# A gated hybrid decoder layer on one core: w2 split at load, attention outputs fetched by background tasks, one more empty turn per attention head

## The chip, the core and the metric

The kernel runs on one core of a Trainium2 chip. The metric is the device time of one execution in microseconds, the median over several; a lower one is better. Engines are named as in the profile: PE is TensorE (with PEld for its weight loads), DVE VectorE, ACT ScalarE, POOL GpSimd and SP SyncE, which here only issues DMAs.

## What is computed

One decoder layer on 256 tokens of width 2048, all in fp32. Two token mixers work side by side: a gated linear attention (branch a) and a causal differential attention of 16 heads (branch b). Cut to what matters:

```python
h = rmsnorm(x, pre_norm_g)
a_q, a_k, a_v, a_g, a_lr, b_q, b_k, b_v, b_g, m_a, m_b = split(h @ w_in)
gk  = log_sigmoid(a_lr @ w2 + gk_b) / 16            # forget gate, w2: 16 x 1024
o_a = rmsnorm(gla_chunked(a_q, a_k, a_v, gk)) * silu(a_g)
o_b = rmsnorm(diff_attention(b_q, b_k, b_v, lam)) * silu(b_g)
y   = sigmoid(m_a) * (o_a @ w_branch_a) + sigmoid(m_b) * (o_b @ w_branch_b)
out = x + rmsnorm(y @ w_out, post_norm_g)
```

## The kernel before

**Products by halves.** Every fp32 operand is split into a high part, rounded to the format that TensorE takes in one pass, and a low part, the remainder. A product is hi·hi + hi·lo + lo·hi. Weights are split as they arrive: SP loads a raw tile of 1 MB (two units), then for each unit ACT writes hi (L298, or L259 for the blocks below) and DVE lo = raw − hi (L299, L260). This runs four units ahead of TensorE (`take` emits the next). The raw tiles, hi and lo come from a pool of three buffers each, so a load waits until DVE has finished with a tile three back.

**Stages.** Weights come in chunks, in the order of `schedule()`: v0 to v4 (the values of branch a and, in v0 to v3, the 32 columns of a_lr), k and q, ag (gates of a), dv, bg, dq, dk (branch b), m (merge gates), y00 to y03 (o_a times w_branch_a), y10 to y13 (o_b times w_branch_b), o (w_out). `token_major` (L444) walks a chunk's kt, with tokens' columns as the stationary operand, 12 matmuls of up to 512 columns a unit (L458; 416 columns in v1 to v3, 400 in v4); `channel_major` (L469) does dq and dk (L479, L481). Five pieces of the projection, the sets, are done with seven products in place of eight, each of four units called blocks: 6 matmuls of 512 columns a block (L658). Their weights come in by POOL's DMAs, which add in flight (L211), by DVE adds (L229) and a few SP loads (raw_s, L253). `mixed(n, keys)` strews n blocks evenly among the units of the named chunks; `alone(4)`, which the kernel has had nowhere in use before the change, puts four with no unit between.

**Background tasks.** Everything else is written as Python generators in a list `tasks`. `pump(n)` (L433) advances each of the first n tasks by one turn, up to its next `yield`; `token_major` pumps after each odd unit, and `block_set` after each odd block (L661). What a turn issues on PE stands behind the last product there. The order in each engine's queue is then a scheduler's, by the program's dependences; DMAs made through `fetch` (L724) keep their program order on SP. A DMA at the head of SP's queue that must wait holds all that stand behind it.

**The forget gate** (L506 to L547) is such a task. w2 lies four times in w2_raw, at rows 0, 32, 64 and 96, 128 rows in all. Its first turn splits them: ACT copies rows 0 to 63 into w2_s as high parts (L509), rows 64 to 127 into a tile w2h (L510), and DVE subtracts to get low parts in rows 64 to 127 of w2_s (L511; the profile calls w2_s w_s). The second turn transposes a_lr on PE (L515), and splits it to lrt (ACT L518, L520, DVE L522); the third issues the eight gate matmuls (L530) and copies their results out (ACT L533). The evacuation of a v chunk is L557 on ACT (vh) and L558 on DVE (vl), and frees its banks.

**Attention of branch b** (L991 to L1038) is one task of one head a turn or two: scores (L940, L941), softmax (DVE L945, ACT L951), a `yield`, the difference of the two maps (DVE L957 to L961, tile prob), a `yield`, its transposes (PE L966), and then for the head before: the product with the values (L972 to L974), the norm (ACT L982, DVE L984 to L989), and every second head transposes and a split. Each four heads' result is stored to DRAM as obh_far and obl_far by POOL's DMAs (L1028), as branch a's did as oah_far and oal_far; both are fetched again as the stationary operands of y0 and y1: oah, oal (four tiles each; kt 0, 1 use tile 0, kt 2, 3 tile 1, kt 8 and 9 tile 2, kt 10 and 11 tile 3) and obh, obl (tile kt/4). The tiles come from one pool of 34 buffers ("u").

**Fetches before.** After m12, m13 and the end of all tasks, the eight of oah and oal stand in a row (L1106 to L1109), then y00 to y03; then the eight of obh and obl (L1117 to L1121), then y10.

Of the kernel before, what the change touches and what calls it, by code (L numbers as in the profile page):

```python
# [7 lines left out]
F32R = mybir.dt.float32r  # L8
BF16 = mybir.dt.bfloat16
U8 = mybir.dt.uint8  # L10
AF = mybir.ActivationFunctionType
# [68 lines left out]
def schedule():  # L80

    kinds = {key: kind for key, kind, _, _ in chunk_plan()}
    steps = []
    blocks = [(i, n) for i in range(len(SETS)) for n in range(SLOTS * 4)]

    def regular(*keys):
        steps.extend((key, n) for key in keys for n in range(units(kinds[key])))

    def mixed(n, *keys):
        at = len(steps)  # L90
        regular(*keys)
        r = steps[at:]
        del steps[at:]
        for i, step in enumerate(r):
            steps.extend(blocks[: (i + 1) * n // len(r) - i * n // len(r)])
            del blocks[: (i + 1) * n // len(r) - i * n // len(r)]
            steps.append(step)

    def channels(g):
        return [key for key in kinds if key[:2] in ("dq", "dk") and key[2] == str(g)]  # L100

    order = [key for key, _, _, _ in chunk_plan()]
    def alone(n):
        steps.extend(blocks[:n])
        del blocks[:n]

    regular(*order[: order.index("v4")])
    mixed(SLOTS * 4, *order[order.index("v4") : order.index("ag0")])
    regular(*order[order.index("ag0") : order.index("dq10")])
    mixed(18, *channels(1))  # L110
    mixed(18, *channels(2))
    mixed(18, *channels(3))
    mixed(14, "m12", "m13")
    mixed(4, "y00")
    mixed(28, *(f"y0{g}" for g in range(1, 4)))
    mixed(12, "y10", "y11")
    regular("y12", "y13", *(f"o{g}" for g in range(4)))
    assert not blocks
    return steps
# [26 lines left out]
def hybrid_kernel(ctx: ExitStack, tc, xt, xn, preg, postg, w, w2, gkb, glag, lamv, diffg, ident_d, causal_d, lmask_d, out):  # L146
# [12 lines left out]
    def u(shape, name, dtype=F32):  # L159
        count[0] += 1  # L160
        return big.tile(shape, dtype, tag="u", name=f"{name}_{count[0]}")
# [17 lines left out]
    def f32(ap):  # L179
        return ap.bitcast(F32)  # L180
# [176 lines left out]
    def load_constants():  # L357
        for i in range(4):
            tc.keep_in_program_order(sp.dma_start(w2_raw[32 * i : 32 * i + RANK, :], w2))
        tc.keep_in_program_order(sp.dma_start(ident, ident_d))  # L360
        for t, src in ((gkb_s, gkb), (glag_s, glag), (diffg_s, diffg), (causal, causal_d)):
            tc.keep_in_program_order(sp.dma_start(t, src))
        tc.keep_in_program_order(sp.dma_start(lam_s, lamv.partition_broadcast(P)))
        yield
        for n in range(0, len(LEVELS) + 2, 4):
            m = min(4, len(LEVELS) + 2 - n)
            t = u([P, 4, S], "lmask")
            tc.keep_in_program_order(sp.dma_start(t[:, :m, :], lmask_d[:, n : n + m, :]))
            pool.tensor_copy(lmask[:, n : n + m, :], t[:, :m, :])
            yield  # L370
# [58 lines left out]
    DONE = object()  # L429
    done = set()  # L430
    latest = [None]

    def pump(n=1):  # L433
        with tc.issue_after(latest[0]):
# [9 lines left out]
    def token_major(key, n, ops, step=1, groups=1):  # L444
        banks = [[ps(tag), ps(tag)] for tag in ("mm", "bg")[:groups]]
        spots = [(g, b) for g in range(groups) for b in range(2)]
        rows = 2 // groups
        for q in range(KT // rows):
            hi, lo = take(key)
            for w, parts in ((hi, (0, 1)), (lo, (0,))):  # L450
                for j in range(rows):
                    kt = rows * q + j
                    a = ops(kt)
                    for g, b in spots:
                        c = n * (groups * j + g)
                        for part in parts:
                            first, last = kt == 0 and w is hi and part == 0, kt == KT - 1 and w is lo
                            i = pe.matmul(banks[g][b][:, :n], a[part][:, P * b : P * b + P], w[:, c : c + n], start=first, stop=last)  # L458
            latest[0] = i.ins
            if groups == 1 and q % 2:  # L460
                pump(step)
            if groups == 2 and q == KT - 4:
                with tc.issue_after(latest[0]):
                    norm()
            if groups == 2 and q > 10:
                pump()
        return banks if groups == 2 else banks[0]
# [36 lines left out]
    act.activation(ones_r, ones, AF.Copy)  # L504

    def forget_gate():  # L506
        top = u([P, 1024], "w2h", F32R)
        r = slice(64, P)
        act.activation(w2_s[:64, :], w2_raw[:64, :], AF.Copy)  # L509
        act.activation(top[r, :], w2_raw[r, :], AF.Copy)  # L510
        dve.tensor_tensor(out=w2_s[r, :], in0=w2_raw[r, :], in1=f32(top[r, :]), op=ALU.subtract)  # L511
        yield
        bank = ps("bg")
        for b in range(2):
            pe.transpose(bank[:, P * b : P * b + P], lr[:, b, :], ident)  # L515
        top = t2([P, 512], "lrh").bitcast(F32R)
        lrt = sm([P, S], "lrt", F32R, bufs=1)
        act.activation(top[:, :S], bank[:, :S], AF.Copy)  # L518
        for i in (0, 64):
            act.activation(lrt[i : i + 32, :], bank[i : i + 32, :S], AF.Copy)  # L520
            r = slice(i + 32, i + 64)
            dve.tensor_tensor(out=lrt[r, :], in0=bank[r, :S], in1=f32(top[r, :S]), op=ALU.subtract)  # L522
        yield
        for hf in range(2):
            for c in range(2):
                bank = ps("bg")
                for i in range(2):
                    ct = 4 * hf + 2 * c + i
                    o = bank[:, S * i : S * i + S]
                    pe.matmul(o, w2_s[:, P * ct : P * ct + P], lrt, start=True, stop=True)  # L530
                for i in range(2):
                    ct = 4 * hf + 2 * c + i
                    act.activation(gp[hf][:, :, 2 * c + i, :], bank[:, S * i : S * i + S].rearrange("p (b t) -> p b t", b=2), AF.Identity, bias=gkb_s[:, ct : ct + 1])  # L533
            yield
        e = [u([P, 1024], "e") for _ in range(2)]
        z = [t.rearrange("p b c t -> p (b c t)") for t in gp]
        for hf in range(2):
            act.activation(e[hf], z[hf], AF.Abs)
            yield
            act.activation(e[hf], e[hf], AF.Exp, scale=-1.0)  # L540
            yield
        for hf in range(2):
            act.activation(e[hf], e[hf], AF.Ln, bias=1.0)
        for hf in range(2):
            yield
            dve.scalar_tensor_tensor(out=z[hf], in0=z[hf], scalar=0.0, in1=e[hf], op0=ALU.min, op1=ALU.subtract)
        done.add("gate")  # L547
# [176 lines left out]
    def fetch(dst, src):  # L724
        tc.keep_in_program_order(sp.dma_start(dst, src))
# [265 lines left out]
    def diff_attention():  # L991
# [3 lines left out]
        while n < 16 or last or pair:  # L995
            new = None
            if n < 16:
                while not waiting or f"split{waiting[0][0]}{waiting[0][1]}" not in done:
                    yield
                new = diff_scores(waiting[0][0], waiting[0][1], 2 * waiting[0][1] + n % 2, *waiting[0][2:])  # L1000
                n += 1
                if n % 2 == 0:
                    waiting.pop(0)
                yield
                diff_weights(new)
                yield
                turn_weights(new)
            while last and last["uu"] is None and f"set{last['g'] - 1}" not in done:
                yield
# [87 lines left out]
    diff_heads(2)  # L1097
    diff_heads(3)

    for g in (2, 3):  # L1100
        banks = token_major(f"m1{g}", 512, x_ops, 2)
        for b in range(2):
            merge_gate(1, g, b, banks[b])
    while tasks:
        pump()
    oah = [u([P, 2, 2, S], "oah", F32R) for _ in range(4)]  # L1106
    oal = [u([P, 2, 2, S], "oal", F32R) for _ in range(4)]
    for i in range(4):
        fetch(f32(oah[i]), oah_far[i])  # L1109
        fetch(f32(oal[i]), oal_far[i])  # L1110
    for g in range(4):
        banks = token_major(f"y0{g}", 512, a_ops)
        for b in range(2):
            t = t2([P, 512], "part")
            act.activation(t, banks[b], AF.Copy)
            pool.dma_start(part_far[g][:, b, :], t)
    obh = [u([P, 4, S], "obh", F32R) for _ in range(4)]  # L1117
    obl = [u([P, 4, S], "obl", F32R) for _ in range(4)]
    for g in range(4):
        fetch(f32(obh[g]), obh_far[g])  # L1120
        fetch(f32(obl[g]), obl_far[g])  # L1121
    mh = [u([P, 4, S], "mh", F32R) for _ in range(4)]
    ml = [u([P, 4, S], "ml", F32R) for _ in range(4)]

# [186 lines left out]
```

## Time and profile before

| what | value |
|---|---|
| median of three runs | 1130.57 us (1130.39 to 1134.64) |
| profiled execution | 1131.25 us |
| its span | 1129.5 us |
| TensorE busy | 1106.8 us (98%) |
| VectorE, ScalarE busy | 818.6 us, 680.0 us |
| mean granted TensorE clock | 0.996 of full speed |
| moved by DMA | 274.56 MB, 243 GB/s on average |

The profile is of one execution; its times start at the span's start. A row of the timeline has the start, the duration, the engine and line, the operation with the tile written and the tiles read, the shapes, how many such instructions in a row are taken together, and in brackets how long the engine stood idle before it and what it waited for. A DMA's row on SP (SPq) shows when it was issued; the time to its landing is listed apart. Matmuls are pipelined: the time from one start to the next is what one costs, and is shorter than the duration in the row.

### The profile page before, as it was taken

To read this page: it belongs to the slowest core of one execution; us is meant where nothing else is said; L and a number is where in the kernel's file an instruction comes from. 1 tells how busy PE (TensorE), PEld (TensorE's weight loads), DVE (VectorE), ACT (ScalarE), POOL (GpSimd) and SP (SyncE) were. 2 spreads that over 40 slices of the span, in tenths; PEclk is the share of its full clock that TensorE was granted. 3 is DMA by queue.
4 is the path that set the end of the run, shared out by engine and by line. 5 is a ranking of instruction groups with operands and counts; after the bars stand their busy time and mean duration, and the time that the engine had idled before them with its cause. 6 is when DMAs were issued, how large, how long until landed. Compare 5 with 4: busy or idle time off the path is not lost.

```text
span 1129.5 us, 15167 instructions
## 1 busy us (share of the span) xinstructions
PE 1106.8 (98%) x5578; PEld 951.7 (84%) x5578; DVE 818.6 (72%) x1151; ACT 680.0 (60%) x1004; POOL 136.7 (12%) x209
## 2 busy tenths in 40 slices
PE   9989999999999999999999999999999999999997
PEld 8989888888888888888888888887888878888886
DVE  6786769986776577667788888877486767585554
ACT  7768555654545466556677778675456555544451
POOL 0121100010001021112212312122012100000000
PEclk9999999999999999999999999999999999999999
DMA  8789764678566485989788988778779786588552
GB/s 316 258 301 312 213 169 150 223 271 316 194 238 217 147 304 201 376 207 250 224 270 226 244 235 247 223 242 230 310 257 302 205 261 247 206 341 313 188 214 75
DMA packets 55371, 274.56 MB, mean 243 GB/s; under 512 B 6848, under 2 KB 7488, under 8 KB 36608
## 3 DMA queue, kind: packets, MB, share of 16 engines
q1 hardware_dynamic: 33392, 195.97, 48.0%
q0 software_dynamic: 21184, 76.56, 25.6%
q10 hardware_dynamic: 720, 1.06, 0.3%
q8 instruction: 44, 0.72, 0.2%
q14 instruction: 31, 0.25, 0.1%
HBM read 249.44 MB, written 24.12 MB: 242 GB/s over the span
## 4 chain that ended last, share of the span: by engine, by line
PE 92%; DMA 2%; issue 2%; ACT 1%; DVE 1%; POOL 0%; SPq 0%; DVEq 0%; POOLq 0%; ACTq 0%
PE mm L458 45%; PE set L658 16%; PE mm L479 15%; PE mm L481 8%; PE bg L458 2%; DMA oal<-oal_far 1%; PE bg L812 1%; PE mm L441 1%; PE bg L441 1%; PE bg L940 1%; PE bg L941 1%; DMA raw_v<-in_w_dram 1%; DMA obh<-obh_far 1%; PE bg L966 0%; ACT hi L298 0%
## 5 line engine op out<-in xcount | busy, mean ns | idle before, releaser
L458 PE MATMUL mm<-hi,xs 128*128 128x512 f32 (+2 forms) x896 | 216.6, 382 | 1.1 <-ACT hi L298 1.1
L479 PE MATMUL mm<-xs,hi 128*128 128x512 f32 x768 | 197.7, 391 | 0.0
L260 DVE TENSOR_TENSOR lo<-chain,hi 128x1024 fp32r<-128x1024 f32 x120 | 146.7, 1223 | 69.6 <-ACT hi L259 68.4
L458 PEld LDWEIGHTS mm<-hi,xs 128*128 128x128 f32 x896 | 167.7, 190 | 26.5 <-ACT hi L298 1.8
L259 ACT ACTIVATE hi<-chain 128x1024 fp32r<-128x1024 f32 x120 | 127.1, 1060 | 103.7 <-PE mm L458 41.8
L479 PEld LDWEIGHTS mm<-xs,hi 128*128 128x128 f32 x768 | 142.8, 188 | 27.3
L458 PE MATMUL mm<-lo,xs 128*128 128x512 f32 (+2 forms) x448 | 116.0, 378 | 0.0
L481 PEld LDWEIGHTS mm<-xs,lo 128*128 128x128 f32 x768 | 104.8, 190 | 7.5
L299 DVE TENSOR_TENSOR lo<-raw_y,hi 128x1024 fp32r<-128x1024 f32 x64 | 78.1, 1223 | 41.3 <-ACT hi L298 35.1
L481 PE MATMUL mm<-xs,lo 128*128 128x256 f32 x768 | 107.1, 282 | 0.0
L298 ACT ACTIVATE hi<-raw_y 128x1024 fp32r<-128x1024 f32 x64 | 67.7, 1061 | 56.4 <-PE mm L458 37.8
L458 PEld LDWEIGHTS mm<-lo,xs 128*128 128x128 f32 x448 | 83.8, 188 | 13.1 <-DVE lo L299 0.3
L658 PE MATMUL set<-hi,square 128*128 128x512 f32 x320 | 86.8, 393 | 0.0
L211 POOL DMA_DIRECT2D chain<-in_w_dram x56 | 48.8, 881 | 195.0 <-DVE lo L260 112.0
L658 PEld LDWEIGHTS set<-hi,square 128*128 128x128 f32 x320 | 58.2, 189 | 10.1
L658 PE MATMUL set<-hi,xs 128*128 128x512 f32 x240 | 65.5, 394 | 0.0
L298 ACT ACTIVATE hi<-raw_ag 128x1024 fp32r<-128x1024 f32 x32 | 34.0, 1061 | 39.9 <-PE mm L458 35.8
L299 DVE TENSOR_TENSOR lo<-raw_ag,hi 128x1024 fp32r<-128x1024 f32 x32 | 39.1, 1223 | 21.4 <-ACT hi L298 21.2
L458 PE MATMUL mm<-hi,oal 128*128 128x512 f32 x128 | 50.6, 395 | 2.9 <-DMA oal<-oal_far 2.9
L458 PE MATMUL mm<-hi,obh 128*128 128x512 f32 x128 | 50.0, 392 | 3.1 <-DMA obh<-obh_far 2.3
L458 PE MATMUL mm<-hi,oah 128*128 128x512 f32 x128 | 50.3, 393 | 0.0
L299 DVE TENSOR_TENSOR lo<-raw_o,hi 128x1024 fp32r<-128x1024 f32 x25 | 30.6, 1225 | 27.0 <-ACT hi L298 26.8
(273 smaller groups left out, 2062.1 us busy)
## 6 DMA issues: line engine op xcount, KB each, us to landing
chain<-in_w_dram POOLq DMA_DIRECT2D x96, 512.0 KB, 8.1
raw_y<-in_w_dram SPq DMA_DIRECT2D x32, 1024.0 KB, 6.5
raw_ag<-in_w_dram SPq DMA_DIRECT2D x16, 1024.0 KB, 4.9
raw_dq<-in_w_dram SPq DMA_DIRECT2D x16, 1024.0 KB, 5.2
raw_dk<-in_w_dram SPq DMA_DIRECT2D x16, 1024.0 KB, 7.2
raw_o<-in_w_dram SPq DMA_DIRECT2D x16, 1024.0 KB, 4.9
raw_v<-in_w_dram SPq DMA_DIRECT2D x15, 832.0 KB, 6.4
raw_s<-in_w_dram SPq DMA_DIRECT2D x10, 1024.0 KB, 6.7
```

Of the source, the lines that this page charges most:

```text
L211: pool.dma_start(dst, src, accum_op=ALU.add)
L259: act.activation(hi_t, raw, AF.Copy)
L260: dve.tensor_tensor(out=lo_t, in0=raw, in1=f32(hi_t), op=ALU.subtract)
L298: act.activation(hi_t[:, a:b], r, AF.Copy)
L299: dve.tensor_tensor(out=lo_t[:, a:b], in0=r, in1=f32(hi_t[:, a:b]), op=ALU.subtract)
L441: i = pe.matmul(out, lhs, rhs, start=first and n == 0, stop=last and n == len(pairs) - 1)
L458: i = pe.matmul(banks[g][b][:, :n], a[part][:, P * b : P * b + P], w[:, c : c + n], start=first, stop=last)
L479: i = pe.matmul(o, hi[:, c], x_pair(kt), start=kt == 0, stop=kt == KT - 1)
L481: i = pe.matmul(o[:, :S], lo[:, c], x_ops(kt)[0], start=False, stop=False)
L658: i = pe.matmul(bank, a[part], wt[:, 512 * j : 512 * j + 512], start=go, stop=end, skip_group_check=not first)
L812: pe.matmul(o, xk[:, P * c : P * c + P], xq.rearrange("p (b c t) -> p b c t", b=2, c=4)[:, :, c, :], start=i == 0, stop=i == 1)
L940: pe.matmul(banks[m][:, lo:up], q2[:, m, i2, t], kh[:, m, i2, :n], start=True, stop=False)
```

## The change

1. The split of w2 moves from the forget gate's first turn to `load_constants`, right behind the loads: one ACT copy of all 128 rows of w2_raw into w2_s, and one DVE subtract that puts the low part of rows 64 to 127 in place. The gate loses a turn, so its transposes and gate matmuls are issued a turn earlier.
2. oah and oal are fetched by a task, `fetch_a`, one pair a turn, put behind the other tasks ahead of m12 and m13 (which pump two tasks a turn). obh and obl are fetched by `fetch_b`, put in with y03: pairs 0 and 1 from y03's units 4 and 5 on, pairs 2 and 3 once y0 is done.
3. Attention has one more `yield` between `diff_weights` and `turn_weights`: one more turn per head.
4. The order of the blocks: in before, 4 blocks in y00, 28 in y01 to y03 and 12 in y10 and y11; now 32 in y00 to y03 evenly, then 4 alone, then 8 in y10 and y11.

```diff
     mixed(14, "m12", "m13")
-    mixed(4, "y00")
-    mixed(28, *(f"y0{g}" for g in range(1, 4)))
-    mixed(12, "y10", "y11")
+    mixed(32, *(f"y0{g}" for g in range(4)))
+    alone(4)
+    mixed(8, "y10", "y11")
...
         tc.keep_in_program_order(sp.dma_start(lam_s, lamv.partition_broadcast(P)))
         yield
+        r = slice(64, P)
+        act.activation(w2_s, w2_raw, AF.Copy)
+        dve.tensor_tensor(out=w2_s[r, :], in0=w2_raw[r, :], in1=f32(w2_s[r, :]), op=ALU.subtract)
...
         for q in range(KT // rows):
             hi, lo = take(key)
+            place[0] = key, q
...
     def forget_gate():
-        top = u([P, 1024], "w2h", F32R)
-        r = slice(64, P)
-        act.activation(w2_s[:64, :], w2_raw[:64, :], AF.Copy)
-        act.activation(top[r, :], w2_raw[r, :], AF.Copy)
-        dve.tensor_tensor(out=w2_s[r, :], in0=w2_raw[r, :], in1=f32(top[r, :]), op=ALU.subtract)
-        yield
         bank = ps("bg")
...
                 diff_weights(new)
+                yield
                 yield
                 turn_weights(new)
...
+    def fetch_a():
+        for i in range(4):
+            oah[i], oal[i] = u([P, 2, 2, S], "oah", F32R), u([P, 2, 2, S], "oal", F32R)
+            fetch(f32(oah[i]), oah_far[i])
+            fetch(f32(oal[i]), oal_far[i])
+            yield
+
+    def fetch_b():
+        for g in range(4):
+            while place[0] < ("y03", 4 + g) if g < 2 else "y0" not in done:
+                yield
+            obh[g], obl[g] = u([P, 4, S], "obh", F32R), u([P, 4, S], "obl", F32R)
+            fetch(f32(obh[g]), obh_far[g])
+            fetch(f32(obl[g]), obl_far[g])
+            yield
+
+    tasks.append(fetch_a())
     for g in (2, 3):
         banks = token_major(f"m1{g}", 512, x_ops, 2)
...
-    oah = [u([P, 2, 2, S], "oah", F32R) for _ in range(4)]
-    oal = [u([P, 2, 2, S], "oal", F32R) for _ in range(4)]
-    for i in range(4):
-        fetch(f32(oah[i]), oah_far[i])
-        fetch(f32(oal[i]), oal_far[i])
     for g in range(4):
+        if g == 3:
+            tasks.append(fetch_b())
         banks = token_major(f"y0{g}", 512, a_ops)
...
-    obh = [u([P, 4, S], "obh", F32R) for _ in range(4)]
-    obl = [u([P, 4, S], "obl", F32R) for _ in range(4)]
-    for g in range(4):
-        fetch(f32(obh[g]), obh_far[g])
-        fetch(f32(obl[g]), obl_far[g])
+    done.add("y0")
```

**Where the gate's matmuls stand on TensorE.** Before, around the transposes of a_lr in v3 (xs_3 is the tokens' third pair of kt; hi and lo are the split weights of a unit) and at v3's end:

```order
L458 MATMUL mm_109_808<-lo_25_701,xs_2_73 128x416
L458 MATMUL mm_110_809<-lo_25_701,xs_2_73 128x416
L515 MATMUL bg_111_844<-ident_88,lr_34_134 128x128 x2
L458 MATMUL mm_109_808<-hi_26_762,xs_3_74 128x416 x2
...
L458 MATMUL mm_110_809<-lo_31_873,xs_8_79 128x416
L530 MATMUL bg_114_888<-lrt_113_848,w2_s_15_92 128x256 x2
L530 MATMUL bg_115_893<-lrt_113_848,w2_s_15_92 128x256 x2
```

And in the changed kernel, at the end of v2 and behind v3's fourth unit:

```order
L463 MATMUL mm_81_582<-lo_23_653,xs_8_79 128x416
L463 MATMUL mm_82_583<-lo_23_653,xs_8_79 128x416
L514 MATMUL bg_108_796<-ident_88,lr_34_134 128x128 x2
L463 MATMUL mm_111_816<-hi_24_686,xs_1_72 128x416 x2
...
L463 MATMUL mm_112_817<-lo_27_781,xs_4_75 128x416
L529 MATMUL bg_113_852<-lrt_110_800,w2_s_15_92 128x256 x2
L529 MATMUL bg_114_857<-lrt_110_800,w2_s_15_92 128x256 x2
```

The transposes went from behind v3's second unit to ahead of its first, and the gate matmuls from behind v3's eighth unit to behind its fourth.

**SP's queue around the fetches of oah and oal.** Before, all eight stand behind the second load of y00:

```order
L277 DMA raw_m13_6_7263<-in_w_dram 128x2048
L277 DMA raw_y00_0_7309<-in_w_dram 128x2048
L277 DMA raw_y00_2_7350<-in_w_dram 128x2048
L725 DMA oah_660_7374<-oah_far_184_2311 128x1024
L725 DMA oal_664_7378<-oal_far_188_2315 128x1024
L725 DMA oah_661_7375<-oah_far_185_2312 128x1024
L725 DMA oal_665_7379<-oal_far_189_2316 128x1024
L725 DMA oah_662_7376<-oah_far_186_2313 128x1024
```

Now they are strewn among the loads from m12's last on:

```order
L277 DMA raw_m12_6_6937<-in_w_dram 128x2048
L724 DMA oah_621_6917<-oah_far_183_2309 128x1024
L724 DMA oal_622_6918<-oal_far_187_2313 128x1024
L724 DMA oah_624_6982<-oah_far_184_2310 128x1024
L277 DMA raw_m13_0_6986<-in_w_dram 128x2048
L277 DMA raw_m13_2_7105<-in_w_dram 128x2048
L724 DMA oal_625_6983<-oal_far_188_2314 128x1024
L724 DMA oah_641_7093<-oah_far_185_2311 128x1024
L724 DMA oal_642_7094<-oal_far_189_2315 128x1024
L277 DMA raw_m13_4_7193<-in_w_dram 128x2048
```

The first three stand six loads earlier than before, the next three ahead of raw_m13_4; the last pair (not shown) stands between raw_y00_0 and raw_y00_2. oal of the second pair waits for the store of an obh_far to land, as it takes that tile's buffer; the next oal for matmuls of the scores, and the last for the last head's norm on DVE.

**SP's queue around the fetches of obh and obl.** Before, behind the third load of y10:

```order
L277 DMA raw_y10_2_8370<-in_w_dram 128x2048
L277 DMA raw_y10_4_8415<-in_w_dram 128x2048
L725 DMA obh_697_8344<-obh_far_244_3018 128x1024
L725 DMA obl_701_8348<-obl_far_248_3022 128x1024
L725 DMA obh_698_8345<-obh_far_245_3019 128x1024
```

Now:

```order
L277 DMA raw_y03_6_8235<-in_w_dram 128x2048
L724 DMA obh_693_8263<-obh_far_243_3016 128x1024
L724 DMA obl_694_8264<-obl_far_247_3020 128x1024
L724 DMA obh_695_8283<-obh_far_244_3017 128x1024
L724 DMA obl_696_8284<-obl_far_248_3021 128x1024
L277 DMA raw_y10_0_8359<-in_w_dram 128x2048
L253 DMA raw_s4_20_8371<-in_w_dram 128x2048
L277 DMA raw_y10_2_8398<-in_w_dram 128x2048
L724 DMA obh_711_8384<-obh_far_245_3018 128x1024
```

Two pairs moved ahead of y10's first load, and two stand behind its second. The load of set 4's blocks (raw_s4_20), which the four blocks alone use, comes between.

More of the change, by code (lines that the diff above doesn't have):

```diff
@@ L431, in hybrid_kernel @@
     latest = [None]
+    place = [None]
     def pump(n=1):
```

## The prediction

> **What bounds the kernel now.** I read the page first, for the busiest engine, then TensorE's list of waits, then the timelines around each wait that the change could touch. The page's head and busy row:
>
> ```profile
> span 1129.5 us, 15167 instructions
> ...
> PE 1106.8 (98%) x5578; PEld 951.7 (84%) x5578; DVE 818.6 (72%) x1151; ACT 680.0 (60%) x1004; POOL 136.7 (12%) x209
> ```
>
> TensorE works for 1106.8 us of a 1129.5 us span, so only 22.7 us are idle. The change takes no matmul away; all it can win is idle time and matmuls run at a lowered clock. The list of waits (line, what ended the wait, us in total, times, longest) says where:
>
> ```profile
> PE bg L530 <- DVE w_s L511: 3.5, 1, 3.5
> PE mm L458 <- DMA oal<-oal_far: 2.9, 1, 2.9
> PE mm L458 <- DMA obh<-obh_far: 2.3, 1, 2.3
> ...
> PE bg L966 <- DVE prob L961: 1.8, 2, 1.3
> ```
>
> These four belong to the edits. They add up to 10.5 us, before what the clock loses after them.
>
> The profiled execution took 1131.25 us, 1.75 more than its span and 0.68 over the median of the runs (1130.57). I make the sum against 1131.25 and take 0.68 off at the end. Half a per cent, 5.65 us, is about what a measurement of this kernel can tell from no change.
>
> **Splitting w2 at load.** The timeline around the longest wait, TensorE, then ScalarE, then VectorE (start, duration, instruction, count, idle before):
>
> ```profile
> 65.19 1.68 PE L458 MATMUL mm<-hi,xs 128*128 128x416 f32 x8
> 67.47 0.38 PE L515 MATMUL bg<-ident,lr 128*128 128x128 f32 x2
> 80.54 0.91 PE L458 MATMUL mm<-lo,xs 128*128 128x416 f32 x4
> 84.93 1.87 PE L530 MATMUL bg<-lrt,w_s 128*128 128x256 f32 x8 [3.48 <-DVE w_s L511]
> 86.60 2.54 PE L458 MATMUL mm<-hi,xs 128*128 128x400 f32 x8
> 94.67 1.61 PE L458 MATMUL mm<-hi,xs 128*128 128x400 f32 x8
> ...
> 82.57 1.05 ACT L510 ACTIVATE w2h<-w_raw 64x1024 fp32r<-64x1024 f32 x1
> 83.64 1.57 ACT L557 ACTIVATE vh<-mm,rstd 128x208 fp32r<-128x208 f32 x4
> ...
> 74.39 0.43 DVE L522 TENSOR_TENSOR lrt<-bg,lrh 32x256 fp32r<-32x256 f32 x1
> 81.64 0.99 DVE L299 TENSOR_TENSOR lo<-raw_v,hi 128x800 fp32r<-128x800 f32 x1 [0.85 <-ACT hi L298]
> 83.65 1.22 DVE L511 TENSOR_TENSOR w_s<-w_raw,w2h 64x1024 fp32r<-64x1024 f32 x1 [1.02 <-ACT w2h L510]
> 84.91 1.66 DVE L558 SCALAR_TENSOR_TENSOR vl<-mm,rstd,vh 128x208 fp32r<-128x208 f32 x4
> ```
>
> Two ScalarE copies (L509, and L510 behind it) and a VectorE subtract stand in line just ahead of the eight gate matmuls: TensorE is done at 81.45 and starts again 3.48 us later. What follows is slow too, because the clock was lowered in this window. The rows give the window and its length, the busy us of PE, PEld, DVE, ACT and POOL, the granted clock (0.83 or 1.00 here), the DMA share and GB/s:
>
> ```profile
> 66.00:75.00 9.00, 9.00 (x50) 8.86 (x49) 8.79 (x13) 6.12 (x9) 4.51 (x9) 1.00 0.77 242
> 80.00:90.00 10.00, 6.52 (x30) 6.10 (x29) 4.66 (x7) 8.88 (x17) 1.98 (x3) 0.83 1.02 421
> 790.00:800.00 10.00, 8.88 (x32) 7.18 (x33) 2.63 (x3) 3.18 (x3) 0.37 (x1) 0.83 1.03 410
> 920.00:930.00 10.00, 7.72 (x34) 6.09 (x33) 5.36 (x5) 5.75 (x7) 1.13 (x2) 1.00 0.95 349
> 547.48 1.12 PE L481 MATMUL mm<-xs,lo 128*128 128x256 f32 x8
> ```
>
> Eight matmuls of 256 columns take 1.12 us at full clock (the L481 row) and took 1.87 here, 0.75 more; the next eight took 2.54 against 1.61, 0.93 more. The old cost is 3.48 + 0.75 + 0.93 = 5.2 us.
>
> What takes its place? The split itself goes to about 39 us, where ScalarE next stood idle for 1.62 us (`43.85` row below) and TensorE did not wait for it; one copy of about 1.06 us (a 1024-column copy) and one subtract of 1.22 us have room. I cost them at nothing; uncovered, they would cost at most their 2.3 us.
>
> ```profile
> 43.85 1.08 ACT L557 ACTIVATE vh<-mm,rstd 128x400 fp32r<-128x400 f32 x2 [1.62 <-PE mm L458]
> ```
>
> The removed turn pulls the transposes two units earlier (67.47 − 65.19 = 2.28 us a unit), from 67.47 to 62.9, and the eight gate matmuls into the middle of v3, four units later, at about 72.1. Before, lrt was complete 7.35 us after the transposes (74.39 + 0.43 − 67.47). With the same lag it is ready at 70.3; with the later place that its second half now has on VectorE, at up to 71.9. Tight, but in time.
>
> At the seam after v3 another wait is then last: v4 needs the banks that the evacuation of v2 and v3 frees. In before, VectorE's split ended at 82.63. The eight gate matmuls, 1.0 us at full clock, now precede v3's end, so everything there shifts by 1.0: v3 ends at 82.4, the split at 83.6, the first bank comes free one evacuation (1.66/4 = 0.42) later, at 84.0, and the second a little after. TensorE waits about 1.75 us and v4 starts at 84.2 instead of 86.60: 2.4 saved, and 0.93 because no clock dip follows. **Term: 3.4 us gained**; 5.1 if that wait doesn't come, 0.7 if lrt is no earlier than 74.8 and 2.7 us are lost to it.
>
> On the dip stands a rule of the Trainium skill, TensorE: Matmul & The Clock Gate, section "HAM oscillation — how this bites in real kernels": the clock falls to half once TensorE is idle for a window of about 3.4 us. Rows here don't fully agree: the 2.93 us wait was followed by the lowered clock (0.83 in 790 to 800), the 2.28 us one (920 to 930) was not. By the rule alone the 2.93 us wait would lose no clock and the whole sum would be 1.9 us smaller.
>
> **oah and oal as a background task.** The wait, the unit in which it falls, and the unit after:
>
> ```profile
> 787.80 0.39 PE L458 MATMUL mm<-hi,oah 128*128 128x512 f32 x1
> 791.12 0.50 PE L458 MATMUL mm<-hi,oal 128*128 128x512 f32 x1 [2.93 <-DMA oal<-oal_far]
> ...
> 795.33 1.09 PE L658 MATMUL set<-hi,square 128*128 128x512 f32 x4
> 796.71 0.39 PE L458 MATMUL mm<-hi,oah 128*128 128x512 f32 x1
> ...
> 799.43 0.39 PE L458 MATMUL mm<-hi,oah 128*128 128x512 f32 x1
> ```
>
> The first unit of y00 takes 795.33 − 787.80 = 7.53 us, the next 799.43 − 796.71 = 2.72. So this wait costs 4.8, of which 1.9 is clock. The fetches were issued from 775.95 on, all eight together, and took 15.8 us to land:
>
> ```profile
> 766.75 9.10 SPq L277 DMA_DIRECT2D raw_y<-in_w_dram  x2
> 775.95 0.40 SPq L725 DMA_DIRECT2D oah<-oah_far  x1
> 783.01 1.06 ACT L298 ACTIVATE hi<-raw_y 128x1024 fp32r<-128x1024 f32 x1 [1.20 <-PE mm L458]
> oal<-oal_far SPq DMA_DIRECT2D x4, 512.0 KB, 15.8
> raw_y<-in_w_dram SPq DMA_DIRECT2D x32, 1024.0 KB, 6.5
> ```
>
> They now start behind m12's last load, six loads ahead of where they stood, two tiles a turn. The two y loads of the first row above are 9.1 us apart, so that is some 50 us earlier, less what the fetches wait for free tiles; the first two pairs, which y00 needs in its first two units, are both issued ahead of raw_m13_4. The last pair stands only just ahead of raw_y00_2, but its first user is kt 10, five units into y00. **Term: 4.8 gained** (2.9 if the clock still dips for another reason).
>
> The price would be paid on SP, whose queue is in order. raw_m13_4 now stands behind a fetch that waits for the store of an attention output and for a tile the scores hold, raw_y00_2 behind one that waits for the last head's normalisation. Their cover: raw_y00_0 was issued at 766.75 and first read at 783.01, 16.3 us later; a load lands in 6.5, so 9.8 us of delay are free. Attention now ends in m13's fifth unit, about when raw_y00_2's buffer came free anyway. I cost this at nothing; without the cover it is the second rival.
>
> By the Trainium skill, DMA: Bandwidth & Descriptors, section "Queues, rings and completion order", an engine alternates between queue rows packet by packet, while SP has one row. Three fetches ahead of a load add 1.5 MB to that row, by its fabric ceiling of 435 GB/s an estimated 3.6 us. No run yet shows fetches and loads in this order.
>
> **obh and obl as a background task.** The wait and its unit:
>
> ```profile
> 925.63 0.70 PE L458 MATMUL mm<-hi,obh 128*128 128x512 f32 x2 [2.28 <-DMA obh<-obh_far]
> 908.96 10.75 SPq L277 DMA_DIRECT2D raw_y<-in_w_dram  x2
> 919.77 0.42 SPq L725 DMA_DIRECT2D obh<-obh_far  x1
> obh<-obh_far SPq DMA_DIRECT2D x4, 512.0 KB, 9.4
> ```
>
> No dip follows, so it costs 2.3. The first two pairs now stand behind raw_y03_6, three weight loads before their old place (loads come some 10.75 us apart), and land in 9.4: early by far. **Term: 2.3 gained.** New is the stretch of four blocks between y03 and y10 with no unit between. VectorE adds raw_s4_20 into a chain there, soon after that load's issue; if it lands in 5 to 7 us TensorE is not kept, at 8 I count 0.6 lost, at 10 2.6. The loads of this kind take:
>
> ```profile
> DMA to landing us min/median/max: 4.8/6.7/13.8
> ```
>
> I take 0.5 lost, near the median.
>
> **The extra empty turn.** One of the two waits for prob:
>
> ```profile
> 550.12 0.74 PE L966 MATMUL bg<-ident,prob 128*128 128x128 f32 x3 [1.30 <-DVE prob L961]
> ```
>
> A turn is at least one unit of a block, six matmuls of 0.227 us (2.72/12) = 1.4 us, and mostly more; both waits, 1.3 and 0.5, go. **Term: 1.8 gained** (1.3 if the late one stays). Attention ends later, still inside m13.
>
> **Sum.** 3.4 + 4.8 + 2.3 + 1.8 − 0.5 = 11.8. 1131.25 − 11.8 = 1119.4 for a profiled execution; less 0.68, 1118.8.
>
> **The rivals.** *The w2 wait only moves.* VectorE is busy for 8.79 of the 9 us from 66 to 75, and lrt's second half has 0.2 to 1.8 us of margin. If it comes at 74.8, the term is 0.7: 1121.5. For it: the small margin; against it: the transposes do come 4.5 us earlier. Chance 0.13.
>
> *Slower: weight loads late behind the fetches.* If fetches and loads mix as the eight did and each load behind a fetch needs 15.8 us to land instead of 6.5, and SP is held about 6 us more by the attention's last steps, then 15.8 + 6 − 16.3 = 5.5 us are lost at each of three places (raw_m13_4, raw_y00_2 and raw_y10_4), each with 1.9 of clock: 3 × 7.4 = 22.2, against 11.8 gained: 1141.0. (One place alone would leave 1126.2.) It decides from a delay of 9.8 us on. Against it: never more than three fetches stand together in front of a load ahead of y00, and their waits end with attention, not after it. Chance 0.05.
>
> *The waits return smaller.* The tasks run so late that y00 or y10 still waits for its pair, and the block stretch loses 2.6: 11.8 − 4.8 − 2.1 = 4.9 gained, 1125.7. In effect the change then doesn't do what it says. Against it: the order has the fetches of the first two pairs clearly ahead. Chance 0.09.
>
> *More than I count*, the seam after v3 costing nothing: 1130.57 − (5.1 + 4.8 + 2.3 + 1.8) = 1116.6, and something unseen beyond it. Chance below 1115.5: 0.05.
>
> **How the numbers follow.** The forecast, 1118.8, has 0.68, and its own range is 1116 to 1121.5. Faster by over 0.5% (below 1124.9): 0.68 + 0.13 + 0.05 = 0.86; within 0.5%: 0.09; slower: 0.05. The range 1115.5 to 1123.5 takes in the forecast and the first rival with the unknown ends, and leaves out the others, not quite 2 in 10.
>
> **What would show it.** In the changed profile: no wait of L529's matmuls for w_s, and one of 1 to 2 us at v4's first matmuls for VectorE or ScalarE; y00's first unit in about 2.7 us with no wait for oal; none for obh at y10; none of over 0.5 us for prob; the clock at 1.00 around 80 and 790 us. TensorE idle about 13 us in all in place of 22.7. I am wrong if a wait for hi of L298 or L259 of several us appears in m13, y00 or y10, or if L529 waits for lrt.

## The result and the profile after

The changed kernel takes 1120.88 us (median, 1120.05 to 1122.19) against 1131.82 us for the kernel before on the same chip; the ratio is 0.9901, with a 95% interval of 0.9877 to 0.9926. The forecast was 1118.8 us with a range of 1115.5 to 1123.5. The profiled execution took 1120.19 us, 11.06 less than that of before.

TensorE's list of waits in the changed kernel (line, what ended the wait, us in total, times, longest):

```profile
PE mm L463 <- ACT hi L298: 1.9, 3, 0.8
PE set L657 <- DVE lo L260: 1.9, 1, 1.9
PE mm L463 <- DVE vl L557: 1.7, 1, 1.7
...
PE bg L939 <- ACT kh L920: 0.2, 1, 0.2
```

All four waits that the edits aimed at are gone. Two are new: 1.7 us for the evacuation (vl) and 1.9 us for a block's low half (lo). TensorE is busy for 1103.1 us of a span of 1118.4, so 15.3 us are idle in place of 22.7; the prediction said about 13.

The first edit, in TensorE's timeline and then VectorE's:

```profile
62.43 1.76 PE L463 MATMUL mm<-hi,xs 128*128 128x416 f32 x8
71.58 1.10 PE L529 MATMUL bg<-lrt,w_s 128*128 128x256 f32 x8
83.46 1.78 PE L463 MATMUL mm<-hi,xs 128*128 128x400 f32 x8 [1.71 <-DVE vl L557]
90.77 1.61 PE L463 MATMUL mm<-hi,xs 128*128 128x400 f32 x8
```

```profile
71.02 0.43 DVE L521 TENSOR_TENSOR lrt<-bg,lrh 32x256 fp32r<-32x256 f32 x1
82.97 1.22 DVE L557 SCALAR_TENSOR_TENSOR vl<-mm,rstd,vh 128x208 fp32r<-128x208 f32 x3
```

lrt is complete at 71.45 and the gate matmuls start at 71.58, without a wait. v4's first matmul then waits 1.71 us for the bank that VectorE frees. The split of w2 itself now runs at 37.5 us on ScalarE and 41.2 us on VectorE, and TensorE has no wait there.

The first unit of y00, and the stretch between y03 and y10, on TensorE:

```profile
782.50 0.39 PE L463 MATMUL mm<-hi,oah 128*128 128x512 f32 x1
785.23 1.07 PE L657 MATMUL set<-hi,square 128*128 128x512 f32 x4
...
907.66 1.07 PE L657 MATMUL set<-hi,square 128*128 128x512 f32 x4
910.62 0.74 PE L657 MATMUL set<-lo,square 128*128 128x512 f32 x2 [1.89 <-DVE lo L260]
911.20 0.40 PE L463 MATMUL mm<-hi,oah 128*128 128x512 f32 x1
...
913.97 1.07 PE L657 MATMUL set<-hi,square 128*128 128x512 f32 x4
...
920.07 0.39 PE L463 MATMUL mm<-hi,obh 128*128 128x512 f32 x1
```

y00's first unit takes 2.73 us in place of 7.53. obh is there when y10 starts. But the block at 907.66 has its low half 2.05 us late (910.62, where four matmuls of 0.227 us would have ended at 908.57), the two late matmuls take 0.58 in place of 0.45 us, and the four blocks alone take 6.10 us (913.97 to 920.07) in place of 4 × 1.36 = 5.44. In sum 2.8 us are lost there. VectorE shows why, with the load's issue on SP below it:

```profile
901.70 1.23 DVE L299 TENSOR_TENSOR lo<-raw_y,hi 128x1024 fp32r<-128x1024 f32 x1 [0.59 <-ACT hi L298]
908.20 1.23 DVE L229 TENSOR_TENSOR chain<-chain,raw_s 128x1024 f32<-128x1024 f32 x1 [5.28 <-DMA raw_s<-in_w_dram]
909.34 1.22 DVE L260 TENSOR_TENSOR lo<-chain,hi 128x1024 fp32r<-128x1024 f32 x1
```

```profile
883.52 0.58 SPq L724 DMA_DIRECT2D obh<-obh_far  x1
891.29 0.33 SPq L277 DMA_DIRECT2D raw_y<-in_w_dram  x1
898.87 0.33 SPq L253 DMA_DIRECT2D raw_s<-in_w_dram  x1
```

raw_s4_20 is issued at 898.87 and landed at 908.2, 9.3 us later. The add that needs it stands at the head of VectorE's queue for 5.28 us, and the split that TensorE is waiting for stands behind it. The granted clock is 1.00 in every window where it had been lowered (window, its length, busy us of the five engines, clock, DMA share, GB/s):

```profile
80.00:90.00 10.00, 8.29 (x43) 7.45 (x42) 5.22 (x8) 8.94 (x18) 1.41 (x2) 1.00 1.03 370
786.00:796.00 10.00, 10.00 (x46) 8.28 (x45) 6.74 (x7) 5.64 (x6) 0.55 (x1) 1.00 0.69 245
```

**The gain by stretches.** v3's first unit in the kernel before:

```profile
62.93 1.68 PE L458 MATMUL mm<-hi,xs 128*128 128x416 f32 x8
```

It now starts 0.5 us earlier (62.43, with the 0.13 us of transposes already ahead of it: 0.6). v4's third unit starts at 90.77 for 94.67, 3.9 earlier, so 3.3 belong to the gate. Up to y00 the gain is 787.80 − 782.50 + 1.36 = 6.7, as one more block stands ahead of y00 now. So the stretch between, nearly all of it attention, brought 2.8. Of these, 2.5 stand in the lists of waits. Besides the 1.8 for prob, attention waited in the kernel before for

```profile
PE bg L941 <- DVE kl L922: 0.4, 2, 0.2
PE bg L940 <- ACT kh L921: 0.3, 1, 0.3
PE bg L1016 <- DVE ogb L989: 0.2, 1, 0.2
```

and of these 0.9 us only the 0.2 for kh are left. y00's first unit brings 4.8, the stretch between y03 and y10 takes back 2.8, and obh brings 2.3: 0.6 + 3.3 + 2.8 + 4.8 − 2.8 + 2.3 = 11.0 of 11.06.

### The profile page after: what moved, and what is told of

The parts are those of the page before. It is cut to its first block, busy times and chain, and to the rows that moved or that the text cites. A ratio compares the mean times of both kernels' runs of the same rounds, so it can differ in the third digit from the quotient of the medians.

```text
span 1118.4 us, 15160 instructions
## 1 busy us (share of the span) xinstructions
PE 1103.1 (99%) x5578; PEld 947.6 (85%) x5578; DVE 817.2 (73%) x1151; ACT 677.4 (61%) x1003; POOL 136.2 (12%) x209
## 4 chain that ended last, share of the span: by engine, by line
PE 93%; issue 2%; DVE 2%; DMA 1%; ACT 1%; POOL 0%; SPq 0%; DVEq 0%; POOLq 0%; ACTq 0%
PE mm L463 47%; PE set L657 16%; PE mm L484 15%; PE mm L486 8%; PE bg L463 2%; PE mm L445 1%; PE bg L811 1%; DMA raw_s<-in_w_dram 1%; PE bg L445 1%; PE bg L939 1%; PE bg L940 1%; DMA raw_v<-in_w_dram 0%; DVE lo L260 0%; PE bg L965 0%; ACT hi L298 0%
## 5 line engine op out<-in xcount | busy, mean ns | idle before, releaser
L299 DVE TENSOR_TENSOR lo<-raw_y,hi 128x1024 fp32r<-128x1024 f32 x64 | 78.1, 1223 | 37.5 <-ACT hi L298 37.5
L657 PE MATMUL set<-lo,square 128*128 128x512 f32 x160 | 49.8, 392 | 2.0 <-DVE lo L260 1.9
L657 PEld LDWEIGHTS set<-hi,xs 128*128 128x128 f32 x240 | 43.8, 188 | 7.6
```

The lines of the kernel that those rows point to most:

```text
L299: dve.tensor_tensor(out=lo_t[:, a:b], in0=r, in1=f32(hi_t[:, a:b]), op=ALU.subtract)
L657: i = pe.matmul(bank, a[part], wt[:, 512 * j : 512 * j + 512], start=go, stop=end, skip_group_check=not first)
```

## The experiments

Ratios are to the kernel before, on the same chip, with 95% intervals. The kernel before has a median of 1131.95 us beside the first four runs, 1133.7 beside the next four and 1132.04 beside the last four.

**Each edit alone.** The first is the diff's w2 part alone.

> Only the first edit: w2 split at load, the gate without its first turn; all else as before. Prediction's theory: 3.4 us faster than before (ratio 0.997); no wait of the gate matmuls for w_s, about 1.7 us of waiting at v4's first matmuls for the evacuation of v2 and v3, clock 1.00 in 80 to 90 us. Rival, the wait only moves to lrt: 0.7 us faster at most, with 2 us or more of waiting for lrt ahead of the gate matmuls.

Measured: 1129.76 us, 0.9982 (0.9969 to 0.9995): 2.0 us won, with 0.6 to 3.5 in the interval. Its waits, and two windows:

```profile
PE mm L461 <- DMA obh<-obh_far: 2.1, 1, 2.1
...
PE mm L461 <- DVE vl L555: 1.7, 1, 1.7
```

```profile
80.00:90.00 10.00, 8.29 (x43) 7.41 (x42) 5.07 (x8) 9.17 (x19) 1.66 (x3) 1.00 1.02 369
918.00:928.00 10.00, 7.87 (x28) 6.03 (x28) 3.71 (x4) 4.69 (x6) 1.13 (x2) 0.83 1.01 385
```

The seam wait of 1.7 us and the clock of 1.00 are as predicted, and nothing waits for lrt. The 3.4 lie at the interval's upper part; the rival's 0.7 at its lower end, but its wait for lrt isn't there. The second window is another matter: after a wait for obh of only 2.1 us the clock fell to 0.83, which it hadn't in the profile before.

Second, `fetch_a` alone:

> Only the second edit's first half: oah and oal fetched two tiles a turn by a task ahead of m12; all else as before. Prediction's theory: 4.8 us faster (ratio 0.9958), y00's first unit in 2.7 us in place of 7.5, clock 1.00 in 790 to 800 us, and no wait of TensorE for hi or lo in m13 or y00. Rival, weight loads late behind the fetches: y00's wait is gone, but waits for hi or lo of 2 us or more in m13 or y00 take its place, so 2 us or less is won.

Measured: 1127.21 us, 0.9953 (0.9935 to 0.9971): 5.3 us won. No wait for oal is left, and TensorE waits for no weight in m13 or y00. y00's first unit takes 2.72 us, and the clock is 1.00 in 790 to 800 us. That is the theory, and the rival's 2 us or less lie outside the interval (3.3 to 7.4 us).

Third, `fetch_b` with the new order of the blocks:

> Only obh and obl as a task, with the new order of the blocks (four alone between y03 and y10); all else as before. Theory from the changed kernel's trace: the 2.3 us wait for obh goes, and about 2.8 us come back in the stretch of the four blocks (a wait of 1.9 us for a block's low half, which stands on VectorE behind the add that waits for raw_s4_20, and 0.7 us of shorter gaps): 0.5 us slower to equal. Rival, the prediction's term (0.5 us lost there): 1.8 us faster.

Measured: 1129.15 us, 0.9973 (0.9957 to 0.9989): 3.1 us won. Neither number, since the run did something that neither theory had in it. The new order of the blocks also put the eight fetches of oah and oal ahead of raw_y00_2 on SP. So the wait for oal (4.8 us) went too, and another came, on TensorE and with its cause on ScalarE and SP:

```profile
798.64 0.50 PE L460 MATMUL mm<-hi,oah 128*128 128x512 f32 x1 [1.49 <-ACT hi L298]
...
797.53 1.06 ACT L298 ACTIVATE hi<-raw_y 128x1024 fp32r<-128x1024 f32 x1 [5.62 <-DMA raw_y<-in_w_dram]
...
775.19 16.35 SPq L277 DMA_DIRECT2D raw_y<-in_w_dram  x3
```

raw_y00_2 stood behind eight fetches (4 MB) and took 22.3 us to land (775.19 to 797.5). That is the prediction's slower rival, but in small: 1.49 us, not 7.4. 2.3 + 4.8 − 1.5 − 2.8 (its own wait for the low half is 2.05 us) = 2.8, against the 3.1 measured.

Fourth, one more `yield`:

> Only the extra empty turn per attention head; all else as before. Prediction's theory: 1.8 us faster, both waits for prob gone (1.3 and 0.5 us). From the changed kernel's trace, where the stretch from dq10 to the end of m13 became 2.5 us shorter: 2.5 us faster, as work that follows late transposes also moved. Rival, those 2.5 us came from the other edits: under 1 us faster.

Measured: 1129.69 us, 0.9981 (0.9966 to 0.9996): 2.2 us won, with 0.5 to 3.8 in the interval. No wait for prob is left, and of those for kl, kh and ogb only 0.2 us for kh. The times alone don't tell 1.8 from 2.5, nor exclude the rival; the eleventh run bears on that again.

**What delays the four blocks.** Fifth, the changed kernel with no block alone:

```diff
-    alone(4)
-    mixed(8, "y10", "y11")
+    mixed(12, "y10", "y11")
```

> The whole change, but none of set 4's blocks alone: 32 in y00 to y03 as changed, then 12 in y10 and y11, each followed by a unit. Theory: the 2.8 us lost between y03 and y10 came of four blocks in a row, where VectorE's add waits for raw_s4_20 ahead of a split that TensorE wants at once; with units between, the wait goes and 2.8 us are won over the changed kernel: about 1118 us, ratio to the kernel before 0.988. Rival, the late landing of raw_s4_20 costs the same wherever it stands: a wait of about 2 us for a low half in y10, ratio as of the changed kernel, 0.990.

Measured: 1117.80 us, 0.9859 (0.9842 to 0.9876). The wait is gone. But this doesn't yet show that blocks in a row are the cause, since raw_s4_20 is now issued at another place and time as well. The next two leave the blocks and move only the fetches. Sixth:

```diff
-            while place[0] < ("y03", 4 + g) if g < 2 else "y0" not in done:
+            while place[0] < ("y03", g) if g < 2 else "y0" not in done:
```

> The whole change, but the first two pairs of obh and obl are issued two weight loads earlier (behind y03's second load). Theory: raw_s4_20 took 9.3 us to land because the four fetches of 2 MB stood in the queues ahead of it (DMA engines fully busy from 886 to 905 us); with the fetches some 16 us earlier it lands in 5 to 7 us and the wait of 1.9 us is under 0.5: 1.5 to 2 us faster than the changed kernel, ratio 0.988 to 0.989. Rival, the load and the blocks' own chain loads fill the engines anyway: landing near 9 us, the wait stays.

Measured: 1118.17 us, 0.9865 (0.9846 to 0.9883). Its raw_s4_20 on SP, the add on VectorE, and the blocks on TensorE:

```profile
899.59 0.33 SPq L253 DMA_DIRECT2D raw_s<-in_w_dram  x1
...
904.38 1.23 DVE L229 TENSOR_TENSOR chain<-chain,raw_s 128x1024 f32<-128x1024 f32 x1 [0.74 <-DMA raw_s<-in_w_dram]
...
912.45 1.07 PE L657 MATMUL set<-hi,square 128*128 128x512 f32 x4
917.89 0.39 PE L463 MATMUL mm<-hi,obh 128*128 128x512 f32 x1
```

The load lands in 4.8 us, and the four blocks take 917.89 − 912.45 = 5.44, not a tenth too long. So the idea that four in a row cost 0.7 by themselves is wrong: that too came from the late load. With the load in time, the four blocks alone cost nothing.

Seventh, all fetches behind raw_s4_20:

```diff
-            while place[0] < ("y03", 4 + g) if g < 2 else "y0" not in done:
+            while "y0" not in done:
```

> The whole change, but all four pairs of obh and obl are fetched only once y0 is done, behind raw_s4_20 and y10's second load. If the fetches delay raw_s4_20: it lands in 5 to 7 us and the wait for the low half goes; if not, it stays at 1.9 us. Either way the wait for obh comes back at y10's first unit, as the fetch takes 9 to 13 us and is issued some 8 us ahead of use: 2 to 6 us, with up to 2 us of lowered clock: 1122 to 1127 us.

Measured: 1118.89 us, 0.9873 (0.9851 to 0.9894). The load and the add:

```profile
898.93 0.33 SPq L253 DMA_DIRECT2D raw_s<-in_w_dram  x1
907.84 0.37 SPq L724 DMA_DIRECT2D obh<-obh_far  x1
...
903.88 1.23 DVE L229 TENSOR_TENSOR chain<-chain,raw_s 128x1024 f32<-128x1024 f32 x1 [0.90 <-DMA raw_s<-in_w_dram]
...
917.24 0.39 PE L463 MATMUL mm<-hi,obh 128*128 128x512 f32 x1
```

The load lands in 5.0 us and the wait for the low half is gone; but the wait for obh that I expected didn't come. The first obh was issued at 907.84, 9.4 us ahead of its use at 917.24, and the four of obh landed in 6.5 us (median; those of obl in 7.5), not in the 9 to 13 that I had taken from loaded queues.

Twelfth, one pair ahead of the load and the other behind:

```diff
-            while place[0] < ("y03", 4 + g) if g < 2 else "y0" not in done:
+            while place[0] < ("y03", 6 + 0 * g) if g < 2 else "y0" not in done:
```

> The whole change, but only one pair of obh and obl (1 MB) is issued ahead of raw_s4_20, the second behind y10's second load. Half the dose of the fetches: raw_s4_20 landed in 9.3 us behind two pairs, in 5 us behind none. Theory of the backlog: 6.5 to 8 us, a wait for the low half of at most 0.7 us, and 1.5 us or more faster than the changed kernel. Rival, the last chain loads of POOL make it late: landing still near 9 us, wait near 1.9 us.

Measured: 1118.13 us, 0.9877 (0.9860 to 0.9894), beside 0.9900 of the changed kernel on that chip. The load and the add:

```profile
898.90 0.33 SPq L253 DMA_DIRECT2D raw_s<-in_w_dram  x1
...
905.33 1.22 DVE L229 TENSOR_TENSOR chain<-chain,raw_s 128x1024 f32<-128x1024 f32 x1 [2.38 <-DMA raw_s<-in_w_dram]
```

From the issue, the same within 0.1 us in all three, the load took 5.0 us with no pair ahead, 6.4 with one and 9.3 with two (9.5 in the third run, which also has two pairs ahead: issued at 906.95, added from 916.43 on). POOL's chain loads are issued at the same times in the three, within 0.1 us. So the fetches delay the load, and the chain loads alone don't. The spans agree: 1116.2, 1115.6 and 1115.5 us in the sixth, seventh and twelfth runs against 1118.4 in the changed kernel, 2.2 to 2.9 less, where 2.8 were read off that stretch.

**The slower rival.** Eighth, all of oah and oal in one turn:

```diff
             fetch(f32(oal[i]), oal_far[i])
-            yield
+        yield
```

> The whole change, but all eight tiles of oah and oal in one turn: five fetches (2.5 MB) now stand between raw_m13_2 and raw_m13_4, none behind raw_y00_0. Prediction's theory, 9.8 us of free delay on a weight load: raw_m13_4 comes 4 to 6 us later and TensorE doesn't wait for it: time as of the changed kernel, ratio 0.990. Rival, loads late behind fetches: waits for hi or lo of 3 us or more in m13, with lowered clock, 4 us slower or more than the changed kernel.

Measured: 1120.15 us, 0.9882 (0.9864 to 0.9900). No wait for a weight. But raw_m13_4 was issued at 745.39, where the changed kernel has 745.21, so the load was hardly later: the run doesn't reach the point from which the rival decides. The third run is the better test.

**The gate and the turn within the whole.** Ninth, the changed kernel itself, unaltered:

> The changed kernel itself, beside the three others on the same chip, so that they can be set against it. Ratio to the kernel before 0.988 to 0.991, TensorE's wait for a low half behind raw_s4_20 1.9 us, at the seam after v3 1.7 us.

Measured: 1121.15 us, 0.9900 (0.9885 to 0.9915), with waits of 1.6 and 1.7 us. Tenth, the gate's turn kept:

```diff
     def forget_gate():
+        yield
         bank = ps("bg")
```

> The whole change, but the forget gate keeps an empty turn in place of its split: w2 is split at load, transposes and gate matmuls are issued at the old turns. Tells the two halves of the first edit apart. Theory: the split's place is what mattered; lrt is ready at about 74 us, where the order now has the gate matmuls (some five units into v3), so at most 0.5 us of waiting for it, and the seam after v3 waits 1.7 us as before: time as of the changed kernel within 0.5 us. Rival, the earlier turn matters: a wait for lrt of 1 us or more at the gate matmuls.

Measured: 1120.62 us, 0.9896 (0.9881 to 0.9911), equal within the intervals. TensorE and VectorE:

```profile
75.17 0.63 PE L530 MATMUL bg<-lrt,w_s 128*128 128x256 f32 x4
84.23 1.73 PE L463 MATMUL mm<-hi,xs 128*128 128x400 f32 x8 [1.71 <-DVE vl L558]
...
74.51 0.43 DVE L522 TENSOR_TENSOR lrt<-bg,lrh 32x256 fp32r<-32x256 f32 x1
```

lrt is complete at 74.94 and the matmuls start at 75.17: with w2 already split, the scheduler put them just behind lrt here too. The earlier turn brought nothing that can be measured; the earlier split brought the gain. Eleventh, without the extra turn:

```diff
                 diff_weights(new)
-                yield
                 yield
                 turn_weights(new)
```

> The whole change without the extra empty turn per head. Theory: both waits for prob come back and the time is 1.8 to 2.5 us longer than the changed kernel's (ratio higher by 0.0016 to 0.0022). Rival, the stretch from dq10 to m13 became shorter through the fetches' new place: under 0.8 us longer.

Measured: 1122.94 us, 0.9914 (0.9899 to 0.9929), 1.8 us longer than the changed kernel beside it, with 1.8 us of waiting for prob, and the waits for kl and kh back as well:

```profile
PE bg L965 <- DVE prob L960: 1.8, 3, 1.1
...
PE bg L940 <- DVE kl L921: 0.5, 2, 0.2
PE bg L939 <- ACT kh L920: 0.3, 1, 0.3
```

The four times (1122.12 to 1123.42) lie clear of the changed kernel's (1121.06 to 1121.62), which speaks against the rival's 0.8 or less. The turn is thus worth 1.8 us here and 2.2 in the fourth run; the intervals don't tell these apart.

## Why the prediction was right

**The gate: right.** The forecast had lrt ready between 70.3 and 71.9 us and wanted at 72.1; it was ready at 71.45 and used at 71.58. The seam was put at 1.75 us and is 1.71; the gain at 3.4 and is 3.3 in the trace. The rival in which the wait moves to lrt fell by little: 0.13 us of margin. No run delays lrt in this order. In the tenth run lrt comes 3.5 us later, but there the scheduler also put the gate matmuls later, so it says nothing of that margin. What the prediction took for the work of two parts, split and turn, is the work of the split.

**oah and oal: right.** 4.8 us forecast, 4.8 in the trace, 5.3 in the second run.

**The extra turn: right.** 1.8 forecast, 1.8 and 2.2 measured. The stretch with attention gained 2.8 in the two traces. Of the 1.0 beyond, 0.7 are the waits for kl, kh and ogb that the prediction left out: they go in the fourth run, with the turn alone, and those for kl and kh come back in the eleventh, without it. The last 0.3 was not traced to a cause.

**obh and the four blocks: the mechanism right, the size wrong.** The prediction named the add of raw_s4_20 on VectorE, with 0.6 us lost if the load lands in 8 us and 2.6 if in 10. It landed in 9.3, which by this scale is 1.9, as much as the wait in the list; the two late matmuls behind it and the four blocks bring the loss to 2.8. The failed step is "I take 0.5 lost, near the median": a median over ten loads in all stages (6.7 us) stood for one load whose queue the change itself had filled with 2 MB just before. The same edit's own fetches were in the order rows that I showed. With −2.8 in place of −0.5 the forecast would have been 1121.1, against the 1120.88 measured.

**The slower rival: rightly judged unlikely, but its point was set too low.** I let it decide from 9.8 us of delay on. In the third run a load landed 15.8 us later than the usual 6.5 (22.3) and TensorE lost 1.49. I had counted only to ScalarE's reading of the tile, 16.3 us after the issue of another load. In the third run TensorE was free for this unit at 798.64 − 1.49 = 797.15. ScalarE's copy takes some 1.1 us from its start to the first matmul (797.53 to 798.64), so the load had to be there at 796.04, 20.85 us after its issue at 775.19. Less the usual 6.5, 14.3 us of delay were free, not 9.8; 15.8 came, and the rest is the 1.49.

**The clock.** The term for obh assumed that its wait of 2.3 us lowers no clock, as in the one profile before. In all three single-edit profiles that still have the wait it did (0.83 in the first run above, the second and the fourth below). What that adds to the gain in the median was not measured. In the two profiles that the sum compares it plays no part. There the forecast of 11.8 came near the 11.06 measured because errors met, which was luck: the loss at the blocks was put 2.3 too low, and the gain 1.0 too low in attention and 0.6 too low ahead of the gate. The 0.6 have come 9 us into the span, long before the first edit's split at 37.5 us: the matmul that waits for its weights there starts at 9.14 in the kernel before, at 8.50 in the changed one and at 8.89 in the ninth run, of the same kernel, so they look like scatter.

**Two readings.** A row that takes two loads together ends with the issue of the second, so the two y loads that the prediction puts 9.1 us apart are about 8.8 apart, and those at 10.75 about 10.4. No term rests on it.

## What to carry to other kernels

A transfer's time to land is no property of its kind: the same 1 MB load took 5.0, 6.4 or 9.3 us here. When a change moves transfers, take the bytes that the change puts into the queues just ahead of the one you look at, and set the landing by that. A wait at the head of an engine's queue costs what stands behind it, as VectorE's 5.28 us did here: look for the add or the copy that waits for a load ahead of the split that TensorE needs. And moving the fetches by one or two loads, with nothing else altered, was worth 3.0 us of the changed kernel's 1121.15 in the twelfth run, beside it on the same chip. The sixth and seventh runs had no changed kernel beside them; they are 2.0 and 1.3 us faster than the eighth, which is built nearly like it, and the seventh's times overlap with the eighth's.

## What the runs showed of the hardware

**The same wait lowers the clock in one profile and not in another.** The window of 10 us at the wait for obh, in before (2.28 us of waiting), in the second run (2.28) and in the fourth (2.4):

```profile
918.00:928.00 10.00, 7.72 (x34) 6.10 (x33) 5.41 (x5) 5.69 (x8) 1.13 (x2) 1.00 0.76 283
```

```profile
918.00:928.00 10.00, 7.72 (x28) 5.89 (x27) 3.56 (x4) 4.08 (x5) 1.13 (x2) 0.83 1.01 385
```

```profile
924.00:934.00 10.00, 7.61 (x27) 5.97 (x27) 3.68 (x3) 3.55 (x5) 1.13 (x2) 0.83 1.01 385
```

Shorter waits differ as well. The tenth run waits 1.98 us for a block's low half, with this window around it:

```profile
905.00:915.00 10.00, 8.02 (x30) 6.21 (x29) 6.07 (x6) 3.19 (x3) 0.00 (x0) 0.86 0.35 127
```

In the third run the same wait is 2.05 us, and the clock is 1.00 in 915 to 925.

The Trainium skill, TensorE: Matmul & The Clock Gate, section "What's actually happening", says that the window by which the clock is set runs freely, not from the kernel's start. That one wait of 2.28 us has two outcomes fits it; that 2.0 to 2.4 us can suffice doesn't fit the 3.4 us that it gives for the window, and the measurement decides. The lowered clock goes with the scatter of the runs: the kernel before lies between 1128.72 and 1136.09 us over 29 executions, the changed one between 1120.05 and 1122.19 in the first four and 1121.06 and 1121.62 in four more. Of the 29, the fastest has a mean granted clock of 0.997 and the slowest one of 0.992; this half per cent of the span is, as an estimate, 5.6 of the 7.4 us between them. Which waits lower the clock in which execution was not recorded.

**Full DMA engines move different amounts.** In the changed kernel, while POOL's accumulating chain loads were under way and after them:

```profile
886.00:900.00 14.00, 14.00 (x64) 11.58 (x63) 9.79 (x10) 7.92 (x8) 1.76 (x2) 1.00 1.00 280
900.00:904.00 4.00, 4.00 (x19) 3.33 (x18) 2.33 (x2) 2.12 (x2) 0.00 (x0) 1.00 1.04 433
```

The engines are fully busy in both, at 280 and at 433 GB/s. Whether the accumulation is the reason is not shown: no run isolates it.
